# Twelve layouts for the split weight chunks of a two-layer decoder trunk

## The chip, the cores and the metric

The kernel runs on one core of one Trainium2 chip. The metric is device time in microseconds (us) of one execution.

## The reference, cut to what matters

The reference is a decoder trunk of two layers over 256 tokens of width 1024, in float32. In each layer a normalised `h` goes through one wide input projection; three branches use its parts (dilated attention, a gated linear recurrence, a convolution module), their outputs are projected, gated, summed and projected again, and an MLP with a squared ReLU (width 4096) follows. Nearly all arithmetic is matrix products of the 256 tokens with weight matrices.

```python
for l in range(DEPTH):
    h = rms_norm(x, norm_mix_pre[l])
    proj = h @ w_in[l]                       # 1024 x 11776
    ...
    y_a = dilated_attention_mixer(q, k, v, cos, sin, w_o_attn[l])
    y_b = rg_lru_mixer(lru_x, lru_gate, ..., w_o_lru[l])
    y_c = conformer_conv_mixer(glu_in, ..., w_o_conv[l])
    merged = g0 * y_a + g1 * y_b + g2 * y_c
    x = x + rms_norm(merged @ w_out[l], norm_mix_post[l])
    h = rms_norm(x, norm_mlp_pre[l])
    u = jnp.square(jax.nn.relu(h @ w_mlp_up[l]))
    x = x + rms_norm(u @ w_mlp_down[l], norm_mlp_post[l])
```

## The kernel before

**Weights come in chunks.** All weights are streamed in 92 chunks per layer, 184 in all, in the order that `chunk_plan` (L47) gives: 64 per layer are weight-stationary (kinds `ws`, `rope`, `oa`) and 28 are activation-stationary (`as`: the value projections `v`, `wo`, `ua` and `dn`). A chunk is 128 partitions by 2048 float32 words. `weights` (L497) brings one chunk in: a DMA of 1 MB on SP's queue into a `raw` buffer (two of them), and then, in two halves of 1024 words, `split` (L488): ScalarE casts the half to the narrower float32r format, the high part `whi`, and VectorE subtracts that from the raw words, the low part `wlo`. The buffers `whi` and `wlo` are two separate rings of three buffers each (`NHI`, L93), so weights are prepared up to three chunks ahead. One chunk is handled otherwise: with `spread`, the last `dn61` of the first layer goes into eight smaller slots.

**Three products for one.** A product of activations and weights is made of three float32r products: high by high, low by high and high by low. In a weight-stationary chunk `ws_items` (L707) loads 128 columns of `whi` or `wlo` as the stationary operand (`hi[:, s]`) and streams 256 tokens of the activations' high part `mh` or low part `ml` past it, into 256 columns of PSUM. One chunk takes 48 such matrix multiplications: for each of its two output blocks first 16 with `whi`, then 8 with `wlo`. In an activation-stationary chunk `as_items` (L881) loads 128 tokens of an activation as the stationary operand and streams 512 words of `whi` or `wlo` past it; such a chunk takes 24 matrix multiplications. The value projections of the second and third head groups (`v1`, `v2`) take every second token as the stationary operand (`slice(t, T, 2)`, L893), that is, words with a step of two; `v0`, `wo`, `ua` and `dn` take contiguous tokens. The attention output is split into `oh` and `ol` with a step of two on the written side (L994).

**The order.** `Sched` (its `run`, L242) is a list scheduler that runs when the program is built: it emits the instructions of every engine in an order that follows from modelled costs, from the data dependencies and from how many buffers of each ring (`RINGS`, L107) are free. The large products keep one fixed order on TensorE (`main`, L479, chains them); the rest is placed around them. Dependencies in `Sched` are kept by first and last element of a region. The waits between engines on the chip are then set by the framework below it from the accesses to each tile.

Of the kernel before, what the change touches and what calls it, by code (L numbers as in the profile page):

```python
# [8 lines left out]
F32R = mybir.dt.float32r  # L9
# [4 lines left out]
P = 128  # L14
T = 256
D = 1024
L = 2
NTAP = 31
EPS = 1e-6
CHUNK = 2048  # L20
# [26 lines left out]
def chunk_plan():  # L47
    q0, k0, v0, lx0, lg0, gl0, br0 = 0, 1536, 3072, 4608, 5632, 6656, 8704
    plan = []

    def ws(name, mat, c0, c1=None):
        plan.append((name, "ws", mat, (c0, c0 + P if c1 is None else c1)))

    for n in ORDER:
        kind, a = n[:2], n[2:]
        if n[0] == "v":
            for kb in range(2):
                plan.append((f"{n}{kb}", "as", "w_in", (kb, v0 + int(n[1]) * 512)))
        elif n[0] in "qk":
            plan.append((n, "rope", "w_in", (q0 if n[0] == "q" else k0) + int(n[1]) * 512 + int(n[2]) * 256))  # L60
        elif kind == "gl":
            ws(n, "w_in", gl0 + int(n[3]) * P, gl0 + D + int(n[3]) * P)
        elif kind == "oa":
            plan.append((n, "oa", "w_o_attn", int(a) * 512))
        elif kind != "lw":
            mat, c0 = {"lx": ("w_in", lx0), "lg": ("w_in", lg0), "ga": ("w_in", br0), "gb": ("w_in", br0 + D),
                       "gc": ("w_in", br0 + 2 * D), "ob": ("w_o_lru", 0), "oc": ("w_o_conv", 0)}[kind]
            ws(n, mat, c0 + int(a) * 256)
    for c in range(2):
        for kb in range(2):  # L70
            plan.append((f"wo{c}{kb}", "as", "w_out", (kb, c * 512)))
    for kb in range(9):
        if kb == 0:
            plan += [(f"ua{k}", "as", "w_mlp_up", (k, 0)) for k in range(2)]
        elif kb < 8:
            ws(f"up{2 * kb}", "w_mlp_up", (2 * kb) * 256)
            ws(f"up{2 * kb + 1}", "w_mlp_up", (2 * kb + 1) * 256)
        if kb > 0:
            for c in range(2):
                plan.append((f"dn{kb - 1}{c}", "as", "w_mlp_down", (kb - 1, c * 512)))  # L80
    return plan


NCH = 92
# [8 lines left out]
NHI = 3  # L93
# [10 lines left out]
LINE = 128  # L104
PSUM_TAGS = ("mm", "tp", "sc")
UNPADDED = PSUM_TAGS + ("st",)
RINGS = ("mm", "tp", "sc", "raw", "whi", "wlo", "upad", "xp", "sm", "pT")  # L107


class Buf:  # L110
    def __init__(self, sch, pool, shape, dt, tag, name):
        self.sch, self.pool, self.shape, self.dt, self.tag, self.name = sch, pool, shape, dt, tag, name
        self.t = None
        self.log = []
        self.left = 0
        self.held = False
        self.uses = []
# [12 lines left out]
    def __getitem__(self, idx):  # L130
        if not isinstance(idx, tuple):
            idx = (idx,)
        reg, n = [], 1
        for i, d in enumerate(self.shape):
            e = idx[i] if i < len(idx) else slice(None)
            if isinstance(e, int):
                reg.append((e, e + 1))
            else:
                r = range(*e.indices(d))
                reg.append((r[0], r[-1] + 1))  # L140
                if i:
                    n *= len(r)
        return View(self, tuple(reg), n, lambda t: t[idx])
# [5 lines left out]
class Part:  # L149
    def __init__(self, buf, off):  # L150
        self.buf, self.off = buf, off

    def __getitem__(self, idx):
        return self.buf[idx[0], idx[1].start + self.off:idx[1].stop + self.off]


class Quarters:
# [38 lines left out]
class Sched:  # L196
# [45 lines left out]
    def run(self):  # L242
# [4 lines left out]

        for tag in RINGS:
            ring, c = self.rings[tag], self.cap[tag]
# [117 lines left out]
def trunk_kernel(ctx: ExitStack, tc: tile.TileContext, x_d, pos_d, w_d, lruw_d, par_d, gain_d, const_d, id_d, out_d):  # L367
    nc = tc.nc
    cp = ctx.enter_context(tc.tile_pool(name="cp", bufs=1))
    wp = ctx.enter_context(tc.tile_pool(name="wp", bufs=1))  # L370
    sp = ctx.enter_context(tc.tile_pool(name="sp", bufs=1))
    pp = ctx.enter_context(tc.tile_pool(name="pp", bufs=1, space=bass.MemoryType.PSUM))
    S = Sched()
# [4 lines left out]
    def slot(name, dt=F32, shape=(P, 2, T)):  # L378
        return S.buf(sp, shape, dt, "s2", name, NSLOT)
# [58 lines left out]
    def dma(eng, out, in_, nbytes):  # L438
        def fn():
            o = out.ap() if isinstance(out, View) else out  # L440
            i = in_.ap() if isinstance(in_, View) else in_
            eng.dma_start(out=o, in_=i)

        e = {id(nc.gpsimd): "POOL", id(nc.scalar): "ACT"}.get(id(eng), "SP")
        o = S.op(e, DMA_ISSUE[e], fn, views(in_), views(out))
        o.dma = nbytes / DMA_RATE / 1e3
        return o
# [40 lines left out]
    def split(hi, lo, src, scale=None):  # L488
        if scale is None:
            return act(hi, src, AF.Copy), tt(lo, src, hi.f32(), OP.subtract)  # L490
        return (act(hi, src, AF.Copy, scale=scale),
                stt(lo, src, scale, hi.f32(), OP.mult, OP.subtract))
# [4 lines left out]
    def weights(l, name, spread=False):  # L497
        c = CIDX[name]
        assert c == used[l], (name, c, used[l])
        used[l] += 1  # L500
        nm = f"{name}_{l}"
        raw = S.buf(wp, (P, CHUNK), F32, "raw", f"raw_{nm}", NRAW)
        if l or c:
            o = dma(nc.sync, raw.all(), w_d[l * NCH + c], CHUNK * P * 4)
            if l == 0 and c in late:
                S.follow(o, late[c])
        else:
            for s in range(2):
                o = dma(nc.sync, raw[:, s * HALF:(s + 1) * HALF], w_d[0][:, s * HALF:(s + 1) * HALF], HALF * P * 4)
                if ORDER[0][0] == "v":  # L510
                    S.follow(o, x1_load)
        if spread:
            hs, ls = [], []
            for q in range(4):
                hs.append(slot(f"whi_{nm}{q}", F32R, (P, 512)))
                ls.append(slot(f"wlo_{nm}{q}", F32R, (P, 512)))
                for o in split(hs[q].all(), ls[q].all(), raw[:, q * 512:(q + 1) * 512]):
                    o.prep = True
            return [(Quarters(hs[2 * s:2 * s + 2]), Quarters(ls[2 * s:2 * s + 2])) for s in range(2)]
        hi = S.buf(wp, (P, CHUNK), F32R, "whi", f"whi_{nm}", NHI)  # L520
        lo = S.buf(wp, (P, CHUNK), F32R, "wlo", f"wlo_{nm}", NHI)
        n = HALF if l == 0 and c < 2 else PREP
        for b in range(0, CHUNK, n):
            for o in split(hi[:, b:b + n], lo[:, b:b + n], raw[:, b:b + n]):
                o.prep = True
        return [(Part(hi, s * HALF), Part(lo, s * HALF)) for s in range(2)]
# [44 lines left out]
    def rstd(s2, name):  # L571
        e = stat(f"e_{name}")
        ts(e.all(), s2[0].all(), EPS, OP.add)
        r = stat(f"r_{name}")
        v = stat(f"v_{name}")
        pool_tt(v.all(), s2[1].all(), e.all(), OP.add, 100)
        pool_tt(r.all(), v.all(), nhalf[:, 0:1], OP.pow, 470)
        return r
# [53 lines left out]
    o = dma(nc.sync, x_sb[:, 0, :], x_d[0:P, :], D * P * 4)  # L632
# [74 lines left out]
    def ws_items(ps, j, w, rhs, nk=8, pitch=P, off=0):  # L707
        hi, lo = w
        a, b = [], []
        for k in range(nk):  # L710
            s = slice(k * pitch + off, k * pitch + off + P)
            mh, ml = rhs(k)
            a.append((ps[:, j, :], hi[:, s], mh, k == 0, False))
            a.append((ps[:, j, :], hi[:, s], ml, False, False))
            b.append((ps[:, j, :], lo[:, s], mh, False, k == nk - 1))
        return a, b

    def ws_mm(ps, w, rhs):
        first = last_main[0]
        for j in range(2):  # L720
            main(*ws_items(ps, j, w[j], rhs))

    for l in range(L):
# [9 lines left out]
        upad, cacc, taps = {}, {}, {}  # L733
# [39 lines left out]
        def glu(i):  # L773
            w = weights(l, f"glu{i}")
            ps = mm_ps(f"glu{i}_{l}")
            gemm(f"glu{i}", w, ps, hr)
            if i % 2 == 0:
                upad[i // 2] = S.buf(sp, (P, 2, 288), F32, "upad", f"upad{i}_{l}", 4)
                memset(upad[i // 2][:, :, 0:30], 0.0)
            u2 = upad[i // 2]  # L780
            th = slot(f"gth{i}_{l}", shape=(P, T))
            act(th.all(), ps[:, 1, :], AF.Tanh, scale=0.5)
            stt(u2[:, i % 2, 30:30 + T], th.all(), 1.0, ps[:, 0, :], OP.add, OP.mult)
            if i % 2 == 1:
                conv_pair(i // 2)
# [148 lines left out]
        sm = {}  # L934
# [134 lines left out]
        mh, ml = {}, {}  # L1069
# [23 lines left out]
        for name in ORDER:  # L1093
            kind, a = name[:2], name[2:]
# [46 lines left out]
        for t in range(2):  # L1141
            nm = f"pm{l}{t}"
            s2, mg, mgg = [], [], []
            for c in range(2):
                s2.append(mean_sq(acc[t, c].all(), f"{nm}{c}"))
                m = slot(f"mgg_{nm}{c}", shape=(P, 512))
                tt(m.all(), acc[t, c].all(), g12[c].all(), OP.mult)
                mgg.append(m)
            r = rstd(s2, nm)
            for c in range(2):  # L1150
                m = 128 * FINE[t]
                for k in range(0, 512, m):
                    v = mgg[c][:, k:k + m]
# [68 lines left out]
        for t in range(2):  # L1222
            nm = f"pd{l}{t}"
# [4 lines left out]
            r = rstd(s2, nm)  # L1228
# [95 lines left out]
```

## Time and profile before

| | us |
|---|---|
| median of 2 runs | 1151.57 (1151.57 to 1151.58) |
| the profiled execution | 1151.4 |
| its span, first to last instruction | 1149.6 |
| TensorE busy | 1130.3 (98% of the span) |
| VectorE busy | 905.1 (79%) |
| ScalarE busy | 721.8 (63%) |
| GpSimd busy | 76.2 (7%) |
| DMA, bytes moved | 209.76 MB, mean 182 GB/s |

A busy time is the union of the recorded durations of an engine's instructions. Matrix multiplications are pipelined, so their recorded durations overlap: what one of them costs is read from the distance between their starts, or from the length of a run of them divided by their number.

### The profile page before, as it was taken

How to read it: one execution, taken by the hardware profiler on the slowest of the kernel's cores; microseconds unless marked ns; L12 is line 12 of the kernel's file. 1: busy time of each engine (PE TensorE's matmuls, PEld its weight loads, DVE VectorE, ACT ScalarE, POOL GpSimd, SP SyncE). 2: the span in 40 equal slices, each digit the busy share in tenths (PEclk: the TensorE clock that was granted, in tenths of full speed). 3: DMA queues.
4: the chain of work that ended last, by engine and by line, in shares of the span. 5: the costliest groups of instructions: out<-in, count | busy, mean ns of one | idle time of the engine just before them, and what ended most of it. 6: DMA issues, size and time to landing. Idle time of an engine off the chain costs nothing.

```text
span 1149.6 us, 20586 instructions
## 1 busy us (share of the span) xinstructions
PE 1130.3 (98%) x8258; PEld 1057.6 (92%) x8258; DVE 905.1 (79%) x1374; ACT 721.8 (63%) x1173; POOL 76.2 (7%) x168
## 2 busy tenths in 40 slices
PE   7999999999999999999999999999999999999995
PEld 6999999998999899989889999999988998989994
DVE  6999999999869865555579999999996789555552
ACT  5779939687665464445568897569676656544441
POOL 1000022111000010000010000221200001000000
PEclk9999999999999999999999999999999999999998
DMA  8654466654345565455465543755534465555540
GB/s 287 240 198 147 147 215 210 205 182 143 125 177 185 194 218 184 183 184 186 181 220 184 178 171 133 236 205 187 192 114 150 159 212 189 208 183 183 187 180 37
DMA packets 37649, 209.76 MB, mean 182 GB/s; under 512 B 6449, under 2 KB 9777, under 8 KB 14130
## 3 DMA queue, kind: packets, MB, share of 16 engines
q1 hardware_dynamic: 32976, 200.05, 49.1%
q0 software_dynamic: 4576, 8.40, 2.3%
q8 instruction: 65, 1.06, 0.4%
q14 instruction: 30, 0.25, 0.1%
q10 hardware_dynamic: 2, 0.00, 0.0%
HBM read 201.08 MB, written 1.05 MB: 176 GB/s over the span
## 4 chain that ended last, share of the span: by engine, by line
PE 93%; DVE 2%; ACT 2%; DMA 1%; issue 0%; POOL 0%; SPq 0%; DVEq 0%; POOLq 0%; ACTq 0%
PE dn L466 15%; PE up L466 14%; PE glu L466 8%; PE q L466 6%; PE k L466 6%; PE v L466 4%; PE gc L466 4%; PE gb L466 4%; PE ob L466 4%; PE oc L466 4%; PE lg L466 4%; PE lx L466 4%; PE wo L466 4%; PE ga L466 3%; PE oa L466 2%; PE ua L466 2%
## 5 line engine op out<-in xcount | busy, mean ns | idle before, releaser
L419 DVE TENSOR_TENSOR wlo_dn<-raw_dn,whi_dn 128x1024 fp32r<-128x1024 f32 (+1 forms) x66 | 75.9, 1190 | 69.4 <-ACT whi_dn L406 69.4
L406 ACT CAST whi_dn<-raw_dn 128x1024 fp32r<-128x1024 f32 (+1 forms) x66 | 64.3, 1021 | 76.8 <-PE dn L466 43.0
L423 DVE SCALAR_TENSOR_TENSOR c<-upad,parh,c 128x256 f32<-128x256 f32 x256 | 110.4, 478 | 0.1
L466 PE MATMUL up<-hh_mlp,whi_up 128*128 128x256 f32 x448 | 110.0, 283 | 0.0
L466 PE MATMUL up<-hl_mlp,whi_up 128*128 128x256 f32 x448 | 109.9, 283 | 0.0
L466 PE MATMUL dn<-whi_dn,uh 128*128 128x512 f32 x256 | 99.8, 390 | 0.0
L466 PE MATMUL dn<-wlo_dn,uh 128*128 128x512 f32 x256 | 99.8, 390 | 0.0
L419 DVE TENSOR_TENSOR wlo_up<-raw_up,whi_up 128x1024 fp32r<-128x1024 f32 x56 | 66.4, 1221 | 42.1 <-ACT whi_up L406 42.1
L413 ACT ACTIVATE cpd<-upad,parh 128x256 f32<-128x256 f32 x224 | 94.5, 499 | 3.5 <-DVE c L419 3.5
L466 PEld LDWEIGHTS up<-hl_mlp,whi_up 128*128 128x128 f32 x448 | 85.9, 192 | 0.5
L466 PEld LDWEIGHTS up<-hh_mlp,whi_up 128*128 128x128 f32 x448 | 85.9, 192 | 0.6
L406 ACT CAST whi_up<-raw_up 128x1024 fp32r<-128x1024 f32 x56 | 56.3, 1050 | 39.2 <-PE dn L466 20.4
L466 PE MATMUL dn<-whi_dn,ul 128*128 128x512 f32 x256 | 70.1, 389 | 0.0
L419 DVE TENSOR_TENSOR cpd<-cpd 128x1024 f32<-128x1024 f32 (+2 forms) x84 | 63.4, 774 | 1.0 <-ACT cpd L413 0.9
L466 PE MATMUL up<-hh_mlp,wlo_up 128*128 128x256 f32 x448 | 62.9, 283 | 0.0
L466 PE MATMUL glu<-hh_mix,whi_glu 128*128 128x256 f32 x256 | 62.8, 283 | 0.0
L466 PE MATMUL glu<-hl_mix,whi_glu 128*128 128x256 f32 x256 | 62.8, 283 | 0.0
L466 PEld LDWEIGHTS up<-hh_mlp,wlo_up 128*128 128x128 f32 x448 | 57.8, 192 | 0.0
L466 PEld LDWEIGHTS dn<-whi_dn,ul 128*128 128x128 f32 x256 | 48.1, 188 | 10.0
L466 PEld LDWEIGHTS dn<-wlo_dn,uh 128*128 128x128 f32 x256 | 48.1, 188 | 9.6
L466 PEld LDWEIGHTS dn<-whi_dn,uh 128*128 128x128 f32 x256 | 48.1, 188 | 9.5
L466 PEld LDWEIGHTS glu<-hh_mix,whi_glu 128*128 128x128 f32 x256 | 49.2, 192 | 0.0
(306 smaller groups left out, 3436.8 us busy)
## 6 DMA issues: line engine op xcount, KB each, us to landing
raw_dn<-w_in_stream SPq DMA_DIRECT2D x32, 1024.0 KB, 4.8
raw_up<-w_in_stream SPq DMA_DIRECT2D x28, 1024.0 KB, 4.8
raw_glu<-w_in_stream SPq DMA_DIRECT2D x16, 1024.0 KB, 4.8
raw_q<-w_in_stream SPq DMA_DIRECT2D x12, 1024.0 KB, 5.0
raw_k<-w_in_stream SPq DMA_DIRECT2D x12, 1024.0 KB, 4.8
raw_v<-w_in_stream SPq DMA_DIRECT2D x11, 1024.0 KB, 4.8
raw_lx<-w_in_stream SPq DMA_DIRECT2D x8, 1024.0 KB, 4.8
raw_lg<-w_in_stream SPq DMA_DIRECT2D x8, 1024.0 KB, 4.8
```

Source lines behind the costliest of these rows:

```text
L406: nc.scalar.copy(out.ap(), in_.ap())
L413: nc.scalar.activation(out.ap(), in_.ap(), func, scale=val(scale), **kw)
L419: lambda: nc.vector.tensor_tensor(out=out.ap(), in0=a.ap(), in1=b.ap(), op=op), [a, b], [out])
L423: lambda: nc.vector.scalar_tensor_tensor(out=out.ap(), in0=a.ap(), scalar=val(s), in1=b.ap(), op0=op0, op1=op1), [a, b] + views(s), [out])
L466: nc.tensor.matmul(out.ap(), lhsT=lhs.ap(), rhs=rhs.ap(), start=start, stop=stop)
```

## The change

`whi` and `wlo` of a chunk become the two parts of one buffer of 2 * 2048 + 32 words, and one ring of three such pairs takes the place of the two rings. Where the parts lie in the pair changes from chunk to chunk. Weight-stationary chunks take turns at twelve layouts: mode `r` (high and low one behind the other, as before, but the moving operand and the output in PSUM are both read or written from the last column to the first), mode `i` (high and low interleaved word by word, so each part has a step of two words), and `ir` (both), each with the pair's start moved by 0, 8, 16 or 24 words. Activation-stationary chunks take turns at three: one behind the other, interleaved, and interleaved with a start moved by 16 words. Over both layers this gives, by counting through the plan, 44 chunks of `r`, 44 of `i` and 40 of `ir` among the 128 weight-stationary ones, and 19 plain and 37 interleaved among the 56 activation-stationary ones (one of the 37 is the chunk that goes through the smaller slots and is not changed).

```diff
--- before.py
+++ after.py
@@ -104,7 +104,7 @@
 LINE = 128
 PSUM_TAGS = ("mm", "tp", "sc")
 UNPADDED = PSUM_TAGS + ("st",)
-RINGS = ("mm", "tp", "sc", "raw", "whi", "wlo", "upad", "xp", "sm", "pT")
+RINGS = ("mm", "tp", "sc", "raw", "whi", "upad", "xp", "sm", "pT")
 
 
 class Buf:
@@ -150,8 +150,46 @@
     def __init__(self, buf, off):
         self.buf, self.off = buf, off
 
+    @property
+    def back(self):
+        return self.buf.back
+
     def __getitem__(self, idx):
         return self.buf[idx[0], idx[1].start + self.off:idx[1].stop + self.off]
+
+
+class Placed:
+
+
+    def __init__(self, buf, mode, part, off):
+        self.buf, self.mode, self.part, self.off = buf, mode, part, off
+
+    def __getitem__(self, idx):
+        a, b = idx[1].start, idx[1].stop
+        if "i" in self.mode:
+            return self.buf[idx[0], 2 * a + self.part + self.off:2 * b + self.off:2]
+        o = self.off + self.part * CHUNK
+        return self.buf[idx[0], a + o:b + o]
+
+    @property
+    def back(self):
+        return "r" in self.mode
+
+
+def kinds():
+    return [p[1] for p in chunk_plan()] * L
+
+
+def placing(n):
+
+    ks = kinds()
+    if n >= len(ks):
+        return "", 0
+    m = sum((k == "as") == (ks[n] == "as") for k in ks[:n])
+    if ks[n] == "as":
+        return (("", 0), ("i", 0), ("i", 16))[m % 3]
+    return (("r", 0), ("r", 8), ("r", 16), ("r", 24), ("i", 0), ("i", 8), ("i", 16), ("i", 24), ("ir", 0), ("ir", 8),
+            ("ir", 16), ("ir", 24))[m % 12]
 
 
 class Quarters:
@@ -517,8 +555,9 @@
                 for o in split(hs[q].all(), ls[q].all(), raw[:, q * 512:(q + 1) * 512]):
                     o.prep = True
             return [(Quarters(hs[2 * s:2 * s + 2]), Quarters(ls[2 * s:2 * s + 2])) for s in range(2)]
-        hi = S.buf(wp, (P, CHUNK), F32R, "whi", f"whi_{nm}", NHI)
-        lo = S.buf(wp, (P, CHUNK), F32R, "wlo", f"wlo_{nm}", NHI)
+        pair = S.buf(wp, (P, 2 * CHUNK + LINE // 4), F32R, "whi", f"wpair_{nm}", NHI)
+        mode, off = placing(l * NCH + c)
+        hi, lo = Placed(pair, mode, 0, off), Placed(pair, mode, 1, off)
         n = HALF if l == 0 and c < 2 else PREP
         for b in range(0, CHUNK, n):
             for o in split(hi[:, b:b + n], lo[:, b:b + n], raw[:, b:b + n]):
@@ -710,9 +749,12 @@
         for k in range(nk):
             s = slice(k * pitch + off, k * pitch + off + P)
             mh, ml = rhs(k)
-            a.append((ps[:, j, :], hi[:, s], mh, k == 0, False))
-            a.append((ps[:, j, :], hi[:, s], ml, False, False))
-            b.append((ps[:, j, :], lo[:, s], mh, False, k == nk - 1))
+            out = ps[:, j, :]
+            if hi.back:
+                mh, ml, out = (v.map(lambda t: t[:, ::-1]) for v in (mh, ml, out))
+            a.append((out, hi[:, s], mh, k == 0, False))
+            a.append((out, hi[:, s], ml, False, False))
+            b.append((out, lo[:, s], mh, False, k == nk - 1))
         return a, b
 
     def ws_mm(ps, w, rhs):
```

## Rows read from the trace of the kernel before

**Rows 1.** Parts 1 and 2 of the page: TensorE's busy time, share and granted clock.

```profile
PE 1130.3 (98%) x8258; PEld 1057.6 (92%) x8258; DVE 905.1 (79%) x1374; ACT 721.8 (63%) x1173; POOL 76.2 (7%) x168
...
PE   7999999999999999999999999999999999999995
...
PEclk9999999999999999999999999999999999999998
```

**Rows 2.** Part 4 of the page: the chain that ended last, by engine.

```profile
PE 93%; DVE 2%; ACT 2%; DMA 1%; issue 0%; POOL 0%; SPq 0%; DVEq 0%; POOLq 0%; ACTq 0%
```

**Rows 3.** The chain in order of time: start us, us, what and how many.

```profile
157.21 5.76 PE gb L466 x48
...
325.94 2.10 PE gc L466 x16
...
417.87 10.91 PE dn L466 x48
...
798.75 11.18 PE v L466 x48
```

**Rows 4.** TensorE in order of time, weight-stationary chunk: start us, us, engine, line, out<-in.

```profile
541.19 0.28 PE L466 MATMUL up<-hh_mlp,whi_up 128*128 128x256 f32 x1
...
542.63 1.12 PE L466 MATMUL up<-hh_mlp,wlo_up 128*128 128x256 f32 x8
...
543.59 0.28 PE L466 MATMUL up<-hh_mlp,whi_up 128*128 128x256 f32 x1
```

**Rows 5.** The same view, value projection (step two) and MLP down projection (contiguous).

```profile
798.58 0.39 PE L466 MATMUL v<-whi_v,hh_mix 128*128 128x512 f32 x1
...
801.37 0.39 PE L466 MATMUL v<-whi_v,hh_mix 128*128 128x512 f32 x1
...
1131.11 0.39 PE L466 MATMUL dn<-whi_dn,uh 128*128 128x512 f32 x1
...
1133.83 0.39 PE L466 MATMUL dn<-whi_dn,uh 128*128 128x512 f32 x1
```

**Rows 6.** Weight loads by shape: busy us, mean ns of one, idle before.

```profile
L466 PEld LDWEIGHTS v<-whi_v,hh_mix 128*128 128x128 f32 x96 | 18.9, 197 | 5.2 <-ACT hh_mix L406 1.5 <-issue 0.4
...
L466 PEld LDWEIGHTS dn<-whi_dn,uh 128*128 128x128 f32 x256 | 48.1, 188 | 9.5
...
L466 PEld LDWEIGHTS up<-hh_mlp,whi_up 128*128 128x128 f32 x448 | 85.9, 192 | 0.6
```

**Rows 7.** ScalarE and VectorE by shape: busy us, mean ns of one, idle before.

```profile
L406 ACT CAST oh<-pv 128x512 fp32r<-128x512 f32 x4 | 2.5, 619 | 2.8 <-PE pv L466 2.8
...
L406 ACT CAST hh_mlp<-pt_mlp 128x512 fp32r<-128x512 f32 x8 | 4.5, 583 | 3.8 <-PE pt_mlp L473 3.8
...
L406 ACT CAST whi_up<-raw_up 128x1024 fp32r<-128x1024 f32 x56 | 56.3, 1050 | 39.2 <-PE dn L466 20.4 <-PE up L466 12.5 <-PE ua L466 4.1
...
L419 DVE TENSOR_TENSOR ol<-pv,oh 128x512 fp32r<-128x512 f32 x4 | 2.8, 690 | 7.5 <-ACT oh L406 7.5
...
L419 DVE TENSOR_TENSOR hl_mlp<-pt_mlp,hh_mlp 128x512 fp32r<-128x512 f32 x8 | 5.3, 686 | 0.5
...
L419 DVE TENSOR_TENSOR wlo_up<-raw_up,whi_up 128x1024 fp32r<-128x1024 f32 x56 | 66.4, 1221 | 42.1 <-ACT whi_up L406 42.1
```

**Rows 8.** Engines by stretch: us, busy (instructions) of each, clock, DMA share, GB/s.

```profile
90.00:136.00 46.00, 46.00 (x386) 46.00 (x385) 43.34 (x70) 43.15 (x73) 0.20 (x2) 1.00 0.39 138
...
136.00:160.00 24.00, 24.00 (x202) 24.00 (x201) 23.74 (x34) 12.25 (x21) 1.00 (x2) 1.00 0.47 165
```

**Rows 9.** Waits over the whole span: us in total, times, longest us.

```profile
ACT whi_dn L406 <- PE dn L466: 43.0, 13, 3.4
...
ACT whi_dn L406 <- PE up L466: 31.8, 12, 2.8
...
ACT whi_up L406 <- PE up L466: 12.5, 11, 1.8
```


## The prediction

> **What bounds the kernel.** I read the busy times first, then the chain of waits by engine, then the chain in order of time, and last the starts of single matrix multiplications. [...] The chain that ended last runs 93% over TensorE [rows 2]. Busy alone would not prove a bound, since recorded durations overlap; the pace does. A weight-stationary chunk takes 5.76 us for 48 matrix multiplications [rows 3], 120.0 ns each, and the starts inside a chunk say the same: 12 in 1.44 us from 541.19 to 542.63, then 8 in 0.96 us [rows 4]. Two activation-stationary chunks take 10.91 us for 48 [rows 3], 227.3 ns each. A chunk pair that keeps this pace waits for nobody, so the time is the number of matrix multiplications by their pace, and a change moves it if it moves the pace.
>
> From the two paces comes the cost of a column: (226.7 - 120.0) / 256 = 0.417 ns, with 226.7 = 2.72 us / 12 from the down projection's starts [rows 5]. Then 256 columns are 106.7 ns, and about 13.3 ns of each matrix multiplication are not columns, at either length. The change alters neither the number of matrix multiplications nor of columns; it alters how operands lie.
>
> **Part by part.**
>
> *Stationary weights with a step of two words (modes i and ir).* 44 + 40 = 84 chunks, 48 loads each, 4032 in all. The trace has such loads: the value projections of the later head groups take every second token as stationary operand, and otherwise do what the down projection does. They take 11.18 us for 48, 232.9 ns against 227.3 [rows 3], and without the seam between chunks 2.79 us for 12, 232.5 against 226.7 [rows 5]. The step costs 5.6 or 5.8 ns, on the path, under a stream of 512 columns. I take 5.8: the columns stay what they are, and the part that is not columns is the same at 256 and 512. That is 4032 * 5.8 ns = 23.4 us. Bounds: nothing, if the step hides behind 256 columns in a way that it does not behind 512, and 9 ns, the largest difference in recorded load durations (197 against 188 ns [rows 6]), 36 us.
>
> [...]
>
> *Moving weights with a step of two (activation-stationary).* 36 chunks by 24 are 864 matrix multiplications of 512 columns. No row shows a float32r moving operand with a step. Lower end: nothing. Middle: the load's price per word, 5.8 / 128 = 0.045 ns, on 512 words, 23.2 ns, 20.0 us in all. Upper end: half pace, 512 * 0.417 = 213 ns more, 184 us. I take nothing: the loads fetch 128 spread words and lose only 5.8 ns, about a ninth of the 53 ns that 128 columns take, so a reader that must deliver only one word a column is nearer to no loss than to half pace.
>
> *Moving operand and output backwards (modes r and ir).* 44 + 40 chunks again, 4032 matrix multiplications of 256 columns. The trace shows none backwards. Ends: a gain of the 13.3 ns that are not columns, if these came from the order of the columns (53.6 us less), nothing, and half pace, 106.7 ns each, 430 us. I take nothing: the words touched are the same and neighbours stay neighbours, as in the forward rows.
>
> *Moved starts* (8, 16, 24 words). All operands of the large products in these rows start on multiples of 32 words but for the odd tokens of the step-two projection, which run at the same pace as the even ones [rows 5]. I take nothing; a load that touches a little more costs at most the 5.8 ns of the step, on 64 chunks (33 in r, 31 in ir) and the 33 moved ones of mode i, 97 * 48 * 5.8 ns = 27 us.
>
> *ScalarE and VectorE.* They write 120 interleaved chunks (84 + 36), two halves each. A cast with a step of two on the written side took 619 ns for 512 words against 583, both out of PSUM [rows 7]: 72 ns per half of 1024, 240 * 72 ns = 17.3 us. The subtraction that reads and writes at a step took 690 against 686 [rows 7]: 8 ns per half, 1.9 us. Neither is on the path: even where ScalarE is fullest it is busy 43.15 of 46 us, and VectorE 23.74 of 24 a little later [rows 8], while a slower TensorE gives each chunk there 48 * 5.8 = 278 ns more, against 144 and 16 ns per chunk that they pay. Cover gone, 17 us would be the most.
>
> *One ring in place of two.* High and low are now freed together, with the chunk's last matrix multiplication. The high cast of the chunk three further on, which already waits for TensorE (13 and 12 times in the down, 11 in the up projections [rows 9]), waits up to 8 * 120 ns = 0.96 us longer behind a weight-stationary chunk. Behind it on ScalarE stand activations and their split, then VectorE's subtraction; two casts and a subtraction, 2 * 1.05 + 1.22 = 3.3 us [rows 7], have two chunks of TensorE, 11 us, to be ready in, and the raw buffer, freed a microsecond later, holds up SP's next load by no more. Nothing. The build's scheduler sees interleaved parts as overlapping and may order some side work otherwise: 2 us either way. DMAs stay the same in number and size.
>
> *Slack.* Around the gates the pace is stretched, 2.10 us for 16 [rows 3], 131 ns. Eleven of the 84 chunks lie there (four in the first layer, seven in the second), 11 * 48 * 5.8 ns = 3.1 us; I let half of it vanish, 1.5.
>
> **Sum**, on the profiled execution, which is 0.2 us under the median: 1151.4 + 23.4 - 1.5 = 1173.3, about 1173 us, 1.9% more.
>
> **The rivals.**
> - *Stepped moving weights cost* (ends slower). Place: the activation-stationary chunks, two thirds of them, on the path. For it: the stationary side pays. Against: one word a column is a lighter demand than a load's. With 20 us: 1193; at half pace 1357. It decides from about 1.5 ns a matrix multiplication on, where 2% is passed.
> - *Reading or writing backwards costs* (slower). Place: every r and ir chunk. For it: no row excludes it; against: the same words, in the same pairs. At 0.045 ns a word, 11.6 ns each, 47 us: 1220; at half pace 1603. [...]
> - *The step is free behind 256 columns*, or the layouts do not reach the loads at all: 1151 to 1154. For it: the load's own record is 192 ns in a 256-column stream, between the other two [rows 6]; the price was seen only behind 512.
> - *A layout gains*: if backward streaming removed the 13.3 ns in the 44 chunks of r, 28 us: 1145 with the step's price.
>
> **How the numbers follow.** Chances: the sum 0.55, stepped moving weights 0.15, backwards 0.13, free 0.13, gain 0.04. A 2% difference, about what a measurement here can tell from no change, is 1174.6 us, just above the sum. The sum's own range is 1163 to 1187, from the loads' upper price and the scheduling; I put 0.30 of its chance below the bound and 0.25 above. Slower: 0.25 + 0.15 + 0.13 = 0.53. Same: 0.30 + 0.13 = 0.43. Faster: 0.04. The range of 8 in 10 goes from 1150, which takes in the free case, to 1200, which takes in the middle price of stepped moving weights; left out are half pace, most of backwards, and the gain.
>
> **What would show it.** In the chain, chunks of mode r keep 5.76 us and those of i and ir take 6.04, layout by layout as they take turns; the interleaved activation-stationary chunks keep 5.45 as the plain ones. Casts into interleaved pairs take some 70 ns longer with TensorE's pace untouched by it. It is wrong if r chunks differ from 5.76, if i and r are alike, if the moved starts differ among themselves, or if the time lies in new waits of TensorE.

## The result and the profile after

The changed kernel takes 1341.01 us (median of 2 runs) against 1151.57: 1.1645 of the time before, 95% interval 1.1595 to 1.1695. The forecast was 1173, with a range of 1150 to 1200.

The page of the changed kernel (busy time, TensorE's busy share and granted clock, the chain by engine) shows the same picture as [rows 1, 2], only longer: TensorE busy all through, its granted clock 0.996 as before, and the chain on it for 98% where it was 93%. No new wait has come in, and the number of matrix multiplications is the same 8258. So the pace has changed, that is, the time from the start of one matrix multiplication to the start of the next.

```profile
PE 1321.6 (99%) x8258; PEld 1072.0 (80%) x8258; DVE 904.5 (68%) x1374; ACT 746.4 (56%) x1175; POOL 75.7 (6%) x168
...
PE   8999999999999999999999999999999999999996
...
PEclk9999999999999999999999999999999999999998
...
PE 98%; DMA 0%; ACT 0%; SPq 0%; DVE 0%; DVEq 0%; POOLq 0%; issue 0%; POOL 0%; ACTq 0%
```

The chain of the changed kernel in order of time (start us, us, what and how many) tells which pace. Each line here is two chunks, and the layouts follow from the plan.

```profile
458.34 16.41 PE dn L504 x48
474.75 11.57 PE up L504 x96
...
514.42 21.76 PE dn L504 x48
536.18 11.43 PE up L504 x96
...
591.91 11.41 PE up L504 x96
603.32 21.78 PE dn L504 x48
...
895.61 2.78 PE v L504 x12
```

Two interleaved down projections take 21.76 to 21.78 us for 48, **453.3 to 453.8 ns each, twice the 227.3 of [rows 3]**; one plain and one interleaved take 16.41. The weight-stationary pairs hardly move: 11.57 us for two of mode i (120.5 ns), 11.43 for two of ir (119.1), 11.41 for two of r (118.9), against 120.0 before. A plain value projection takes 2.78 us for 12.

The other rows have their counterparts too. In the groups by shape of the changed kernel (busy us, mean ns of one, idle before), the casts are longer, since about two thirds of them now write at a step (among the up projection's, chunks of i and ir take 1128 ns a cast and chunks of r 1045), and the subtractions are not [rows 7]; the weight loads keep their means to 1 ns in the up and 12 in the down projection, with a step there or without [rows 6]:

```profile
L504 PEld LDWEIGHTS up<-hh_mlp,wpair_up 128*128 128x128 f32 x896 | 141.4, 193 | 2.4 <-issue 2.2
...
L504 PEld LDWEIGHTS dn<-wpair_dn,uh 128*128 128x128 f32 x496 | 98.3, 200 | 81.4 <-issue 73.5 <-PE dn L504 0.5 <-ACT uh L444 0.2
...
L444 ACT CAST wpair_dn<-raw_dn 128x1024 fp32r<-128x1024 f32 x62 | 67.8, 1126 | 132.9 <-issue 49.0 <-PE dn L504 42.1 <-PE up L504 41.1
L457 DVE TENSOR_TENSOR wpair_up<-raw_up,wpair_up 128x1024 fp32r<-128x1024 f32 x56 | 67.3, 1222 | 89.7 <-ACT wpair_up L444 89.7
...
L444 ACT CAST wpair_up<-raw_up 128x1024 fp32r<-128x1024 f32 x56 | 59.9, 1099 | 97.5 <-PE dn L504 63.9 <-PE up L504 24.0 <-PE ua L504 9.6
```

The cast's waits for TensorE have become longer in sum (41.1 and 42.1 us behind up and down, where [rows 9] had 31.8 and 43.0 for the down projection's), and nobody on the chain waits for them.

### The profile page after: what moved, and what is told of

Same layout as the page of the kernel before. It is cut to its first block, busy times and chain, and to the rows that moved or that the text cites. A ratio compares the mean times of both kernels' runs of the same rounds, so it can differ in the third digit from the quotient of the medians.

```text
span 1339.3 us, 20583 instructions
## 1 busy us (share of the span) xinstructions
PE 1321.6 (99%) x8258; PEld 1072.0 (80%) x8258; DVE 904.5 (68%) x1374; ACT 746.4 (56%) x1175; POOL 75.7 (6%) x168
## 4 chain that ended last, share of the span: by engine, by line
PE 98%; DMA 0%; ACT 0%; SPq 0%; DVE 0%; DVEq 0%; POOLq 0%; issue 0%; POOL 0%; ACTq 0%
PE dn L504 21%; PE up L504 12%; PE v L504 8%; PE glu L504 7%; PE wo L504 5%; PE q L504 5%; PE k L504 5%; PE gc L504 4%; PE ga L504 4%; PE oc L504 3%; PE gb L504 3%; PE lg L504 3%; PE ob L504 3%; PE lx L504 3%; PE ua L504 3%; PE oa L504 2%
## 5 line engine op out<-in xcount | busy, mean ns | idle before, releaser
L504 PE MATMUL dn<-wpair_dn,uh 128*128 128x512 f32 x496 | 198.1, 550 | 0.0
L504 PEld LDWEIGHTS dn<-wpair_dn,uh 128*128 128x128 f32 x496 | 98.3, 200 | 81.4 <-issue 73.5
L504 PE MATMUL up<-hh_mlp,wpair_up 128*128 128x256 f32 x896 | 163.3, 283 | 0.0
L504 PEld LDWEIGHTS up<-hh_mlp,wpair_up 128*128 128x128 f32 x896 | 141.4, 193 | 2.4 <-issue 2.2
L504 PE MATMUL up<-hl_mlp,wpair_up 128*128 128x256 f32 x448 | 109.4, 282 | 0.0
L504 PE MATMUL dn<-wpair_dn,ul 128*128 128x512 f32 x248 | 105.1, 549 | 0.0
L504 PE MATMUL glu<-hh_mix,wpair_glu 128*128 128x256 f32 x512 | 92.0, 282 | 0.0
L504 PEld LDWEIGHTS up<-hl_mlp,wpair_up 128*128 128x128 f32 x448 | 86.7, 193 | 2.4 <-issue 2.2
L504 PE MATMUL v<-wpair_v,hh_mix 128*128 128x512 f32 x192 | 81.3, 570 | 1.1 <-ACT hh_mix L444 1.1
L504 PEld LDWEIGHTS glu<-hh_mix,wpair_glu 128*128 128x128 f32 x512 | 80.3, 193 | 0.0
```

The source lines that it names most:

```text
L504: nc.tensor.matmul(out.ap(), lhsT=lhs.ap(), rhs=rhs.ap(), start=start, stop=stop)
```

## The experiments

**Plain activation-stationary chunks in the changed kernel** undo the one part that the profile points at.

```diff
-        return (("", 0), ("i", 0), ("i", 16))[m % 3]
+        return "", 0
```

> The changed kernel with all activation-stationary chunks laid out plainly (high part, then low part); the weight-stationary chunks keep their twelve layouts and the pair buffers. Theory A (a float32r moving operand with a step of two words streams at half pace, 453 ns against 227 for 512 columns, and this is nearly the whole loss): 864 matrix multiplications give back 864 x 221 to 226 ns = 191 to 195 us, so 1146 to 1150 us. Rival B (the shared pair, its single ring or the waits that it brings make the loss, and the step is only where it shows): well over 1200 us remain.

Measured: 1150.95 us, 0.999 of the time before (0.998 to 1.0). The whole loss is gone: 190.1 us less than the changed kernel, 220 ns for each of the 864 matrix multiplications. Theory A holds; nothing of the size of B is left. Its chain has two down chunks at 11.04 to 11.19 us, not 10.91:

```profile
417.13 11.07 PE dn L504 x48
...
462.39 11.19 PE dn L504 x48
...
507.49 11.04 PE dn L504 x48
```

**Plain weight-stationary chunks in the changed kernel** leave that part alone.

```diff
-    return (("r", 0), ("r", 8), ... ("ir", 24))[m % 12]
+    return "", 0
```

> The changed kernel with all weight-stationary chunks laid out plainly and forward; the activation-stationary chunks keep their three layouts. Theory A: the loss stays, 1341 us and up to 12 us more, because the backward chunks' 118 ns instead of 120 ns is lost as well. Rival C (stepped weight loads or backward streams cost what I had forecast or more, and hide in the sum): 20 to 25 us less, 1316 to 1321 us.

Measured: 1342.14 us, 1.1647 of before (1.1629 to 1.1664). The loss stays; the twelve layouts together weigh about 1 us. C is out: no price of stepped loads or backward streams hides in the sum. The chain shows three single weight-stationary chunks that follow one another in the ring, then two up chunks and the same two down chunks of the doubled pace:

```profile
155.79 5.75 PE k L503 x48
161.54 5.69 PE gb L503 x48
167.23 5.71 PE ob L503 x48
...
475.50 11.39 PE up L503 x96
...
514.88 21.76 PE dn L503 x48
```

The 12 us more of theory A did not come, and these lines say why. All weight-stationary chunks here are plain and forward, yet 5.69 and 5.71 us are 118.5 and 119.0 ns a matrix multiplication, where forward chunks of the kernel before took 120.0. Counted through the ring, and by the distances of starts, the chunks in one of its three buffers run at 119.9 ns and those in the other two at 118.6 and 118.8. So a pace under 120 ns in the pairs is no mark of a backward stream: where the buffer lies gives it too.

**Groups of words.** What does the moving stream want? Here high and low parts alternate not word by word but in groups.

```diff
-        return (("", 0), ("i", 0), ("i", 16))[m % 3]
+        return (("", 0), ("g2", 0), ("g4", 0), ("g8", 0), ("b", 0))[m % 5]
```

For a group layout of `g` words `t.rearrange("p (n h g) -> p h n g", h=2, g=g)[:, part]` takes the place of a slice, and `b` puts `[:, ::-1]` on output and weights.

> The changed kernel, but the activation-stationary chunks take turns at five layouts, some eleven chunks each: plain; high and low interleaved in groups of 2, of 4 and of 8 words; plain with moving weights and output read and written backwards. A slow chunk costs 24 x 226 ns = 5.4 us more. Theory A1 (two neighbouring words are enough): groups of 2, 4 and 8 all near 227 to 233 ns, 1146 to 1155 us in all. Theory A2 (lines of four words: what counts is the words used of a line): groups of 2 near 453 ns, 4 and 8 near 227, some 60 us more, 1205 us. Theory A3 (only one unbroken run streams at full pace): groups of 2, 4 and 8 all near 453 ns, some 180 us more, 1326 us. Backward: 227 to 232 ns if the direction does not matter, 453 ns (60 us more) if only a step of plus one is fast.

Measured: 1210.44 us, 1.0505 (1.0484 to 1.0526), theory A2 to within 6 us; the backward chunks, at 233 ns, belong with the fast ones. In its chain the first line is a chunk of groups of 4 and one of 8, the second a backward and a plain one, the third one of groups of 2 and one of 4:

```profile
432.33 11.15 PE dn L528 x48
...
455.05 11.18 PE dn L528 x48
...
477.86 16.47 PE dn L528 x48
```

Groups of 4 and 8 run at 232 ns, like the plain chunk in the second line; groups of 2 take the 453 ns of the step (16.47 us less a group-of-4 chunk, 24 * 232 ns = 5.57, is 10.90 us for 24). So it is not the step as such.

**The same groups, moved by two words.**

```diff
+        return (("", 0), ("", 2), ("g4", 2), ("g8", 2), ("g2", 2))[m % 5]
```

> As the run with groups of 2, 4 and 8 words, but the activation-stationary chunks take turns at plain; plain moved by 2 words; groups of 4 moved by 2; groups of 8 moved by 2; groups of 2 moved by 2. Theory L (the moving stream keeps full pace only where it uses whole lines of four words that start on 16 bytes): plain moved 227 to 233 ns, since it runs through whole lines all the same; groups of 4 moved by 2 lie half in each of two lines and fall to 453 ns, groups of 8 moved by 2 fall too, wholly or in part; groups of 2 stay at 453 ns; 1265 to 1330 us. Rival W (any four neighbouring words will do, wherever they start): only the groups of 2 at 453 ns, 1210 us as before.

Measured: 1293.61 us, 1.1235 (1.1203 to 1.1268), inside theory L's bounds and far from W's 1210. The chain's lines are a moved group-of-4 chunk with a moved group-of-8 one, a moved group-of-2 one with a plain one, and (second layer) a plain one with a moved plain one:

```profile
442.81 18.77 PE dn L528 x48
...
473.09 16.54 PE dn L528 x48
...
1083.81 11.08 PE dn L528 x48
```

By the distances of starts, 18.77 us are 24 * 453 ns for the moved groups of 4 and 24 * 329 ns for those of 8. A line is here what theory L calls one, four words that start on a multiple of 16 bytes. Groups of 4 that straddle two lines fall to the pace of the step; of 8, whose words lie 2, 4 and 2 in three lines, I estimate that half the words pay: 256 * 0.417 + 256 * 0.833 + 13.3 = 333 ns. A plain run moved by two words uses whole lines all along and stays fast, 233 ns. The estimate behind this, from the 0.417 ns of a column in the kernel before and the paces of these two runs, is that a word of a line that is used whole costs one column time, 0.417 ns, and a word of a line that is used in part costs two. It holds to 3% here: it gives 333 ns where 329 were measured, and 512 * 0.833 + 13.3 = 440 where 453 were.

**A step of four words**, to see whether the price is by lines or by words.

```diff
+        if self.mode == "q":
+            o = 4 * (a % HALF) + 2 * (a // HALF) + self.part
+            return self.buf[idx[0], o:o + 4 * (b - a) - 3:4]
...
```

Further lines of the edit give the layouts to the chunks and halve the width.

> The changed kernel with other layouts: weight-stationary chunks take turns at plain and at a step of four words (forward, no moved starts); of the down projection's chunks 8 have moving weights with a step of four words, 7 have a step of two and use only the first 256 of their 512 columns (their other half is left out), all other activation-stationary chunks are plain. Theory A2 (the stream waits for lines of four words, so the pace is set by the words used of a line): step four 4 x 227 = 907 ns, 8 x 24 x 677 ns = 130 us more than the plain 1157 us, 1287 us. Rival F (any step costs a factor of two and no more): 453 ns, 1200 us. For 256 columns at step two: 240 ns if the whole of 120 ns doubles, 227 ns if only the columns' 106.7 ns do. Step-four weight loads: 120 ns a matrix multiplication if a load hides whatever its step, over 125 ns if its lines are paid for.

Measured: 1547.05 us, 1.3428 (1.3404 to 1.3453), far above both figures, for a reason that neither had: the loads. The chain line is a plain down chunk and one of step four; the rows after it, from TensorE in order of time, are the first starts of a half-width chunk at step two and of the chunk that follows, and two starts inside an up chunk whose loads have a step of four; the last is the group of loads:

```profile
588.68 16.52 PE dn L512 x48
```

```profile
621.93 2.00 PE L512 MATMUL dn<-wpair_dn,uh 128*128 128x256 f32 x8
...
627.41 2.05 PE L512 MATMUL dn<-wpair_dn,uh 128*128 128x512 f32 x8
```

```profile
672.45 0.40 PE L512 MATMUL up<-hl_mlp,wpair_up 128*128 128x256 f32 x1
...
673.85 0.40 PE L512 MATMUL up<-hl_mlp,wpair_up 128*128 128x256 f32 x1
```

```profile
L512 PEld LDWEIGHTS up<-hh_mlp,wpair_up 128*128 128x128 f32 x896 | 196.7, 260 | 1.4 <-issue 1.0
```

Moving operands at step four take (16.52 - 24 * 0.227) / 24 = 461 ns, not 907: rival F, one word of a line costs the same factor of two as two words did (453). At 256 columns a matrix multiplication at step two takes 5.48 / 24 = 228 ns, near the 227 of doubled columns with the 13.3 ns beside them paid once; at 512 columns it takes 453, which is twice the whole. What becomes of the 13.3 ns is therefore not settled. The stationary side is another matter: six matrix multiplications in 1.40 us, 233 ns where 120 was the pace, 113 ns more for a load that takes one word from each line. Over 64 * 48 loads that is 347 us, which with 44 us for the moving chunks makes up the measured time to 1 us from the 1157 that I took for plain chunks, and to 5 us from the 1151 of the first experiment.

**Contiguous tokens in the value projections** test the row on which I had priced the step in the load.

```diff
-            src = lambda kk, t: hk(h, kk, slice(t, T, 2) if g else slice(t * P, (t + 1) * P))
+            src = lambda kk, t: hk(h, kk, slice(t * P, (t + 1) * P))
```

> The kernel before, where the value projections of the second and third head groups take contiguous tokens as stationary operand (other tokens than the reference's, so the attention is not the reference's). Theory S (the step in the load costs the 5.8 ns that I priced it at): these projections fall from 233 to 227 ns, 192 x 6 ns = 1.1 us in all. Rival P (the pace there comes from something else, where the buffers lie or how the reads fall together): they stay at 233 ns.

Measured: 1151.45 us in a single run. The total settles nothing, since runs of the kernel before lay between 1151.19 and 1154.18; the pace does. The chain's value projection falls from the 11.18 us of [rows 3] to the down projection's 10.91. Theory S holds for this place: taking the step away gives 5.6 ns back.

```profile
799.29 10.91 PE v L466 x48
```

**Backward alone, in the kernel before**, for the 118 ns that I had not expected.

```diff
-            a.append((ps[:, j, :], hi[:, s], mh, k == 0, False))
...
+            mh, ml, out = (v.map(lambda t: t[:, ::-1]) for v in (mh, ml, ps[:, j, :]))
+            a.append((out, hi[:, s], mh, k == 0, False))
...
```

> The kernel before with one edit: in weight-stationary chunks the moving operand and the output run from the last column to the first; separate rings, no pair, no step. Theory D (the direction alone gives the 118 ns of the backward chunks): 6144 x about 2.2 ns = 13.5 us less, 1138 us. Rival E (the pair's placement gives it, not the direction): 120 ns a matrix multiplication and 1151 us, the same.

Measured: 1142.28 us, 0.9914 of before (0.9899 to 0.9928): below both kernels, by 0.9% of the time before. D holds for this kernel, in which no buffer was moved, though with 9.9 us and not 13.5; E is not refuted for the pairs, where the plain forward chunks above ran at 118.6 and 118.8 ns in two of the three buffers and at 119.9 in the other. Two up chunks take 11.36 us, 118.3 ns each, so the gain is 1.7 ns, 10.4 us over 6144; down and value projections keep their pace.

```profile
425.91 11.36 PE up L466 x96
437.27 10.88 PE dn L466 x48
...
792.41 11.20 PE v L466 x48
```

**Backward everywhere** adds `[:, ::-1]` to the activation-stationary products.

> The kernel before with moving operand and output backward in all large products, weight-stationary and activation-stationary. Theory D (backward moves the pace by some 2 ns a matrix multiplication wherever the moving operand is read): 1142 us as with the weight-stationary ones alone, less 1344 x 2 ns = 2.7 us, 1139.5 us. Rival E2 (the gain belongs to the weight-stationary form; backward activation-stationary chunks ran at 233 ns in the pairs): 1142 to 1150 us.

Measured: 1149.91 us, 0.9982 (0.9973 to 0.999). Rival E2: the activation-stationary pairs go from 10.88 to 11.20 us and give nearly all of it back.

```profile
426.48 11.36 PE up L466 x96
437.84 11.20 PE dn L466 x48
```

**Pairs without the extra 32 words**, all weight-stationary chunks backward at start 0, the others plain, ask why plain chunks in the pairs ran at up to 234 ns.

```diff
-        pair = S.buf(wp, (P, 2 * CHUNK + LINE // 4), F32R, "whi", f"wpair_{nm}", NHI)
+        pair = S.buf(wp, (P, 2 * CHUNK), F32R, "whi", f"wpair_{nm}", NHI)
```

> The changed kernel with all activation-stationary chunks plain, all weight-stationary chunks backward at start 0, and pairs of 4096 words without the 32 extra, so that the three pairs start at the same place modulo 16 KB. Theory G (the 232 to 234 ns of plain chunks in the pairs come from starts that differ from pair to pair): 227 ns in all of them and 118 ns in the others, 1142 us as with backward alone in the kernel before. Rival H (sharing one buffer makes them 232 ns): 1147 to 1149 us.

Measured: 1142.68 us, 0.9917 (0.9902 to 0.9932), as with backward alone. Theory G: with the pairs a whole 16 KB apart plain chunks are back at 226.7 ns, so where the buffers start moved the pace by up to 3% (226.7 to 234), and sharing one buffer and one ring cost nothing (1142.68 us against 1142.28 with two rings). The weight-stationary layouts, which this edit changes too, are not the reason: with the padding and all of them plain and forward (the second experiment), plain down chunks still ran at 228 to 234 ns.

```profile
425.98 11.36 PE up L503 x96
437.34 10.88 PE dn L503 x48
```

## Why the prediction was wrong

**The frame was right.** The time was the pace times the number of matrix multiplications, before and after; no wait, queue or ring decided anything.

**The step that failed is the term for moving weights with a step of two, of which the prediction says "I take nothing".** The price was the end that I had named and put aside: half pace, 453.8 against 227.3 ns, 864 * 226.5 ns = 195.7 us. The argument for nothing compared the stream with the loads, which take 128 spread words at a loss of 5.8 ns. The runs show that loads and streams are charged differently. Behind 256 columns a load at step two was nearly free (120.5 ns a matrix multiplication, against 119.2 to 120.0 without a step) and one at step four cost 113 ns (233). A stream of 512 columns ran at about half pace wherever it used every line of 16 bytes in part only: 453 ns at step two, 461 at step four, 453 for groups of two and for groups of four that straddle lines, against 232 for aligned groups of four and 227 for a plain run; moved groups of eight, with half their words in such lines, ran at 329. Why a stream is charged so is open. A row of one operand side was no neighbour for the other. I had no row of a float32r moving operand with a step, only two ends 184 us apart, and gave the upper one a part of a 0.15 chance; the range left it out.

**The loads' 23.4 us were not there.** The 5.8 ns are real behind 512 columns of contiguous weights, and the experiment on the value projections shows that they go with the step (11.18 to 10.91 us for 48). They do not belong to it alone: the same 233 ns is the pace of plain chunks that stream backward, and of those whose start is moved by two words, with no stepped load in either. What these share is open. Carried over to 256 columns the 5.8 ns vanish: mode i takes 120.5 ns, against 120.0 in the kernel before and 119.2 on average for plain forward chunks in the same pairs. That is 1 to 3 us over its 44 chunks, and ir is no slower than r. The measured price lies near the bound of nothing, and the argument for 5.8, that what is not columns is the same at both widths, did not hold.

**Backward streams gain instead of costing nothing**, 1.7 ns in the weight-stationary chunks of the kernel before. In the changed kernel little of the gain is theirs: r chunks take 118.6 ns on average by the distances of starts, plain forward ones in the same pairs 119.2. Half pace, the largest price in the list, is excluded. The output in PSUM was written backward there too, within the 118.3 ns; in activation-stationary products, where weights and output ran backward together, it came to 6.6 ns, 3%.

**The sum again**: 195.7 us for the stepped streams; backward chunks at 118.9 ns, 4032 * 1.1 = 4.4 us less (direction and place together); mode i 1 us more; plain chunks at some 231 ns, 19 * 24 * 4 = 1.8 us more; 194 in all, against 189.4 measured. The rest, 5 us less, fits the chain's smaller share of other engines (7% before, 2% after): a slower TensorE covers stalls that it used to wait out. Added up over the distances of TensorE's starts in the two traces, the activation-stationary products take 193.6 us more, not 197.5, and the other, small products 1.8 us less. Part of that is pace, since most stepped chunks take 452 to 453 ns and not 453.8; how much is stalls that a slower TensorE covers is argued, not tested.

**What hid, hid.** ScalarE is busy 24.6 us longer (forecast 17.3), VectorE not at all, and neither shows in the time. The single ring cost nothing (1142.68 us without the extra words, 1142.28 with two rings). The moved starts cost nothing in sum (the twelve layouts together weigh about 1 us), but they are not alike: r chunks moved by 8 or 24 words ran at 117.8 ns in the main, those moved by 16 at 120.0 (I had counted 64 moved chunks of r and ir; there are 63). With that, and with r chunks at 5.70 us where 5.76 was forecast, two of the prediction's own signs of being wrong are there, each worth a few us; the 195.7 us lie outside all of them.

## What to carry to other kernels

Before an operand's layout is changed, ask which operand it is: here a row of stationary loads, 5.8 ns for a step of two, did not price a moving stream, 226.5 ns. If two parts must share a buffer, interleave them in aligned groups of 16 bytes, which ran at the pace of a plain run here (232 ns), not word by word (453). When the only bounds of a term are nothing and half pace on the engine that sets the time, the range must hold both or the argument needs a row of the same operand.

## What the hardware showed beyond that

- Streaming a weight-stationary product backward, output and moving operand both, took 118.3 ns in place of 120.0, and 0.9914 of the kernel's time; in activation-stationary products it took 233 in place of 227. The place of the buffers did as much without any change of direction: with pairs 16,512 bytes apart, forward chunks took 118.6, 118.8 or 119.9 ns by buffer. Why is open for both.
- A change of the buffers' pitch from 16,384 to 16,512 bytes moved plain chunks from 226.7 to between 227 and 234 ns, by buffer: two of the three at 232 to 234, the third at 227 to 229.
- A float32r weight load that takes one word from each 16-byte line cost 113 ns more a matrix multiplication of 256 columns (233 for 120).
